# Three pooling inputs and three mixed values of a hybrid decoder layer turned by 32x32 blocks on VectorE and a DRAM detour on GpSimd's DMA queue

## The chip, the cores and the metric

One core of one Trainium2 chip runs the whole program. The metric is the device time of one execution in microseconds (us). The kernel before has a median of 1524.18 us over 3 runs (1524.03 to 1524.83). Everything is float32 at the input and the output.

## What is computed

One layer of a decoder trunk on 256 tokens of 2048 channels. A normalised input is projected into nine parts; two causal mixers work on them, a gated linear attention with 16 heads and a trailing mean over 2, 4, 8 or 16 tokens (one window for each quarter of the channels). Both are gated, summed, projected and added to the input; a gated MLP follows. The part that the change touches:

```python
proj = jnp.einsum('bsd,de->bse', rmsnorm(x, norm_mix_w[l]), w_in[l])
q, k, v, z, b_raw, a_raw, p_in, g_a, g_b = jnp.split(proj, splits, axis=-1)
...
o = gated_delta_rule(q, k, v, g_log, beta)
y_a = rmsnorm(o, gdn_norm_w[l]) * silu(z)
pooled = causal_multiscale_pool(p_in)          # mean over the last 2, 4, 8 or 16 tokens, minus the token
y_b = einsum('bsgc,gcd->bsgd', pooled, pool_w[l]) * pool_scale[l]
mixed = sigmoid(g_a) * y_a + sigmoid(g_b) * y_b
x = x + mixed @ w_out[l]
```

## The kernel before

**Matmuls in split precision.** The program is a long row of matrix products whose weights come from DRAM. A weight tile has 128 partitions and 2 x 512 columns (512 KB). SyncE's queue loads it into `raw` (four buffers). ScalarE casts it to a high part `whi` (L357, three buffers), VectorE subtracts that from `raw` and so makes the low part `wlo` (L368, three buffers). `gemm_a` (L404) then issues twelve matmuls of 128x512 on the tile: for each of two blocks of 128 input channels and each half of the tokens, high times high, low times high, and high times low (L416 to L418). A gemm over all 2048 input channels is eight such tiles, called steps; its result stands in two PSUM tiles, one for each 128 tokens, tokens on the partitions. `weights` (L241) keeps two tiles ahead: when TensorE is given tile n, the loads, casts and splits up to n + 2 have been written.

**The head groups.** The loop at L1245 goes over four groups of 512 channels. Each group has, in this order: K and Q projection (with a scheme that shares products between two column blocks), V, P (the input of the pooling, L1287), gate B, z, the product with `pool_w`, gate A, and the first steps of the next K. The attention's recurrence runs beside them, a piece after each half step (`side`).

**Work that waits for its turn.** What is to be done with a gemm's result is put into the list `later`, and `gemm_a` empties it within the next gemm, ahead of step `flush` (L409 to L411; step 1 in most, step 3 in K and Q). The mixed values have a list of their own, `mixing` (L1235, filled at L1420), which goes into `later` behind K and then Q of the next group. A framework then sets the order on each engine by a simulated timeline; only some stretches are ordered by hand. On the chip each engine works through its list strictly in order.

**The pooling input.** `evict` writes the P gemm, scaled by the norm, to `ev`, tokens on the partitions. The running sums need the tokens along the free axis and the product needs channels on the partitions, so `pooled` (L1306) first turns `ev`: `turned` (L497) makes eight TensorE transposes of 128x128 (L505) into two PSUM tiles `psg`, and two ScalarE copies (L1311) bring them to `pu`. VectorE adds shifted copies (L1319, into `pb` and `pa` in turn, with ScalarE copying the first few tokens, L1318), finishes the mean (L1322 to L1325, `pool`), and the result is split into `phi` (L1327) and `plo` (L1329). For group 3 the windows are applied by matmuls with band matrices instead (`banded`, L1292).

**The mixed values.** `gated` leaves the mixed values of a group in `sz`, tokens on the partitions. The output projection needs channels there. `mixed` (L1413) turns `sz` by eight more transposes, and splits what stands in PSUM into `mhi` (ScalarE, L1416) and `mlo` (VectorE, L1417), one half at a time. For groups 0 to 2 this happens in the next group, for group 3 at the end of the mixers.

**Queues.** Weights go on SyncE's queue (SP). GpSimd (POOL) issues few DMAs in this part of the program and computes a few small things, among them the powers `nk` and `ro` for the norms.

## Time and profile before

| | before |
|---|---|
| median of 3 runs | 1524.18 us (1524.03 to 1524.83) |
| profiled execution, its own time | 1524.25 us |
| its span in the profile | 1522.5 us |
| granted TensorE clock, mean | 0.999 |
| TensorE busy | 1513.1 us, 7260 matmuls and transposes |
| VectorE busy | 1287.0 us |
| ScalarE busy | 896.1 us |
| GpSimd busy | 75.0 us, 97 instructions |

The page of the profile gives each engine's busy time, the span in slices, the chain of work that ended last, and groups of instructions by source line. PE is TensorE, PEld its weight loads, DVE VectorE, ACT ScalarE, POOL GpSimd, SP SyncE. In a row by line stand the line, the engine, the operation, output and input tile, the shape, the count; behind the first bar the busy time and the mean nanoseconds of one; behind the second the idle time ahead of these instructions, and what ended it. In a timeline each row begins with the start and the length in us; `x3` at its end means three such in a row, and a bracket holds the idle time before it and what ended it. A row of DMA issues has the count, the size of one and the median time from issue to landing. In the view by stretch each row has the stretch, its length, the busy time of each engine with its number of instructions, the clock, the share of the DMA engines and the GB/s.

### The profile page before, as it was taken

The numbers are of one execution on the slowest core, as the hardware profiler recorded it, in microseconds if no ns is written. First come the engines' busy times: TensorE is split into PE (matmuls) and PEld (weight loads), VectorE is DVE, ScalarE is ACT, GpSimd is POOL, SyncE is SP. The second block draws the span as 40 slices with busy tenths as digits, with TensorE's granted clock in tenths as the row PEclk, the third lists the DMA queues.
The fourth block names the chain that finished last, engine by engine and source line by source line (L and its number), as shares of the span: only waits on it lengthen the run. The fifth ranks groups of instructions, "written<-read, shape, count | busy, mean of one in ns | idle before, by whom it ended". The sixth has DMA issues, their size and how long they took to land.

```text
span 1522.5 us, 20282 instructions
## 1 busy us (share of the span) xinstructions
PE 1513.1 (99%) x7260; PEld 1250.8 (82%) x7260; DVE 1287.0 (85%) x1799; ACT 896.1 (59%) x1160; POOL 75.0 (5%) x97
## 2 busy tenths in 40 slices
PE   9999999999999999999999999999999999999998
PEld 8888888888878888888888888888888888888886
DVE  6779868888688878888777999999998886989896
ACT  7456556455646456456465676667666665555562
POOL 1000001000100001000000000000000011010100
PEclk9999999999999999999999999999999999999999
DMA  8777647784677747774678656666457468566662
GB/s 277 209 226 221 207 139 225 235 255 115 198 221 218 227 127 219 214 238 154 217 227 303 198 164 218 221 212 216 152 164 238 142 212 276 172 223 219 220 220 100
DMA packets 170099, 313.62 MB, mean 206 GB/s; under 512 B 23650, under 2 KB 27010, under 8 KB 169870
## 3 DMA queue, kind: packets, MB, share of 16 engines
q1 hardware_dynamic: 160864, 283.17, 59.0%
q0 software_dynamic: 7344, 27.27, 5.5%
q10 hardware_dynamic: 1790, 1.89, 0.4%
q8 instruction: 57, 0.93, 0.2%
q14 instruction: 44, 0.36, 0.1%
HBM read 303.33 MB, written 8.95 MB: 205 GB/s over the span
## 4 chain that ended last, share of the span: by engine, by line
PE 98%; DVE 1%; issue 1%; ACT 0%; POOL 0%; POOLq 0%; DVEq 0%
PE psg L455 28%; PE psm L418 14%; PE psm L416 14%; PE psm L417 14%; PE psm L1644 8%; PE psg L1644 7%; PE psm L455 4%; PE psm L606 1%; PE psm L1712 1%; PE psg L505 1%; PE psg L993 1%; DVE wlo L368 1%; PE psg L995 0%; PE psm L521 0%; PE psg L1139 0%
## 5 line engine op out<-in xcount | busy, mean ns | idle before, releaser
L357 ACT CAST whi<-raw 128x1024 fp32r<-128x1024 f32 x400 | 419.9, 1052 | 311.0 <-PE psm L417 157.9
L368 DVE TENSOR_TENSOR wlo<-raw,whi 128x1024 fp32r<-128x1024 f32 x398 | 484.1, 1220 | 119.3 <-ACT whi L357 113.9
L357 ACT CAST whi<-quad 128x1024 fp32r<-128x1024 f32 x217 | 227.9, 1053 | 167.5 <-PE psg L455 46.2
L368 DVE TENSOR_TENSOR wlo<-quad,whi 128x1024 fp32r<-128x1024 f32 x217 | 263.4, 1220 | 39.9 <-ACT whi L357 34.8
L416 PE MATMUL psm<-whi,xhl 128*128 128x512 f32 x384 | 150.0, 391 | 0.0
L417 PE MATMUL psm<-whi,xhl 128*128 128x512 f32 x384 | 149.9, 390 | 0.0
L418 PE MATMUL psm<-wlo,xhl 128*128 128x512 f32 x384 | 139.0, 393 | 0.0
L455 PE MATMUL psg<-whi,fhl 128*128 128x512 f32 x504 | 127.1, 389 | 0.0
L284 DVE TENSOR_TENSOR quad<-quad,quad 128x1024 f32<-128x1024 f32 x92 | 111.9, 1217 | 0.1
L455 PEld LDWEIGHTS psg<-whi,fhl 128*128 128x128 f32 x504 | 94.6, 188 | 19.7
L416 PEld LDWEIGHTS psm<-whi,xhl 128*128 128x128 f32 x384 | 72.1, 188 | 15.0
L417 PEld LDWEIGHTS psm<-whi,xhl 128*128 128x128 f32 x384 | 72.1, 188 | 14.9
L418 PEld LDWEIGHTS psm<-wlo,xhl 128*128 128x128 f32 x384 | 71.7, 188 | 14.6
L455 PE MATMUL psg<-wlo,fhl 128*128 128x512 f32 x252 | 69.8, 389 | 0.0
L455 PE MATMUL psg<-whi,ups 128*128 128x512 f32 x216 | 58.1, 391 | 0.0
L455 PEld LDWEIGHTS psg<-wlo,fhl 128*128 128x128 f32 x252 | 47.3, 188 | 9.9
L1644 PE MATMUL psm<-whi,hhi 128*128 128x512 f32 (+1 forms) x140 | 54.2, 387 | 0.0
L1644 PE MATMUL psm<-whi,hlo 128*128 128x512 f32 (+1 forms) x140 | 53.7, 386 | 0.0
L1644 PE MATMUL psm<-wlo,hhi 128*128 128x512 f32 (+1 forms) x140 | 50.2, 386 | 0.0
L455 PEld LDWEIGHTS psg<-whi,ups 128*128 128x128 f32 x216 | 40.3, 188 | 8.5 <-issue 0.2
L1644 PE MATMUL psg<-whi,hhi 128*128 128x512 f32 (+1 forms) x120 | 46.4, 387 | 0.0
L1644 PE MATMUL psg<-whi,hlo 128*128 128x512 f32 (+1 forms) x120 | 46.1, 386 | 0.0
(495 smaller groups left out, 3001.2 us busy)
## 6 DMA issues: line engine op xcount, KB each, us to landing
raw<-in_w_in_dram SPq DMA_DIRECT2D x212, 512.0 KB, 4.5
raw<-in_w_up_dram SPq DMA_DIRECT2D x104, 512.0 KB, 4.7
quad<-in_w_up_dram SPq DMA_DIRECT2D x72, 512.0 KB, 5.3
raw<-in_w_down_dram SPq DMA_DIRECT2D x56, 512.0 KB, 5.1
quad<-in_w_down_dram POOLq DMA_DIRECT2D x32, 512.0 KB, 5.4
raw<-in_w_out_dram SPq DMA_DIRECT2D x24, 512.0 KB, 3.7
mv<-vrow SPq DMA_DIRECT2D x12, 512.0 KB, 4.9
quad<-in_w_in_dram SPq DMA_DIRECT2D x12, 512.0 KB, 6.8
```

The lines of the kernel that those rows point to most:

```text
L284: nc.vector.tensor_tensor(out_, plus_, minus_, op=ALU.subtract)
L357: last_cast[0] = nc.scalar.copy(hi, raw).ins
L368: last_split[0] = nc.vector.tensor_tensor(lo, raw, hi.bitcast(F32), op=ALU.subtract).ins
L416: mm(ps[:, t, :], lh(k, t), hi[:, kk, :], start=(k == 0), stop=False, **seeded)
L417: mm(ps[:, t, :], ll(k, t), hi[:, kk, :], start=False, stop=False, **seeded)
L418: mm(ps[:, t, :], lh(k, t), lo[:, kk, :], start=False, stop=(k == nk - 1), **seeded)
L455: last_product[0] = mm(ps, lhs(kk), w[n][:, kk], stop=False, skip_group_check=True, start=(first and n == 0 and kk == 0 and lhs is high)).ins
L505: nc.tensor.transpose(pt[:, ff, t * P : (t + 1) * P], src[:, t, f * P : (f + 1) * P], ident)
L606: mm(ps_k0[:, t, :], part(k, t), w[:, kk, :], start=(k == 0 and w is hi and part is xh), stop=(k == KD - 1 and w is lo))
L993: mm(pg0, kq[:, h, 0, 0:P], kq[:, h, :, :], start=True, stop=True)
L1644: mm(ps[:, cs], lhs(kk), part_[:, kk, cs], start=(first and kk == 0 and n == 0), stop=(last and kk == 1 and n == 2), skip_group_check=shared)
L1712: nc.tensor.transpose(out_[f // 2][:, f % 2, t * P : (t + 1) * P], e[:, t, f * P : (f + 1) * P], ident)
```

## The change

A new function turns a tile of 256 tokens x 512 channels without TensorE. VectorE transposes within blocks of 32x32 into `blocks`; one DMA stores `blocks` (512 KB) to a DRAM tile `way`; four DMAs, one for each group of 32 partitions of the target, load the blocks from there in their turned places. All five DMAs are on GpSimd's queue. An element of such a load is a run of 32 floats, 128 bytes, and each load has 32 x 32 = 1024 of them.

```diff
+    def turned_by_dma(src, blocks, dst, queue):
+        nc.vector.transpose(blocks, src)
+        way = dpool.tile([2, P, 512], F32, tag="way", name=nm("way"))
+        queue.dma_start(way.rearrange("t p c -> p t c"), blocks)
+        way = way.rearrange("t (q j) (f a i) -> a j f (t q) i", q=4, a=4, i=32)
+        for a in range(4):
+            queue.dma_start(dst[32 * a : 32 * a + 32].rearrange("j f (u i) -> j f u i", i=32), way[a])
+        return dst
...
         e = evict(ps) if g == 3 else evict(ps, rsh)
+        if g < 3:
+            blocks = mp.tile([P, 2, 512], F32, tag="pa", name=nm("blocks"))
+            u = mp.tile([P, 4, S], F32, tag="pu", name=nm("pu"))
+            turned_by_dma(e, blocks, u, nc.gpsimd)
...
-        def pooled(e=e, g=g, win=win, phi=phi, plo=plo):
-            u = mp.tile([P, 4, S], F32, tag="pu", name=nm("pu"))
-            for f2, pt in enumerate(turned(e)):
-                nc.scalar.copy(u[:, 2 * f2 : 2 * f2 + 2, :], pt)
+        def pooled(u=u, g=g, win=win, phi=phi, plo=plo):
             src, n = u, 1
...
             gated()
+        if g < 3:
+            blocks = mtile(4 + g, [P, 2, 512], F32, nm("blocks"))
+            whole = mp.tile([P, 4, S], F32, tag="sz", name=nm("whole"))
+            turned_by_dma(sz, blocks, whole, nc.gpsimd)
...
         if g < 3:
-            mixing.append(mixed)
+            def parts(whole=whole, mh=mh, ml=ml):
+                nc.scalar.copy(mh, whole)
+                nc.vector.tensor_tensor(ml, whole, mh.bitcast(F32), op=ALU.subtract)
+            mixing.append(parts)
```

In groups 0 to 2 the pooling input is turned right behind its eviction, so `pooled` begins with the sums; and the mixed values are turned as soon as `gated` has written them, into a tile `whole` in the other buffer of `sz`, from which `mhi` and `mlo` are then split as a whole rather than by halves. The buffer of `sz` is also that into which SyncE loads the convolution's taps for V of the next group, and that load moves behind four more weight loads on SyncE's queue. `banded`, and `mixed` of group 3, stay as they are. Line numbers behind the new function are ten higher (L1319 becomes L1329), and some more behind the later edits.

ScalarE's order in group 0, from the last `ga` of the attention's preparation to the split of the pooled values (`whi` are weight tiles, `pu` the turned pooling input, `pb` the first sum, `phi` the high part of the pooled values). Before:

```order
L357 CAST whi_1282<-raw_1280 128x1024
L1015 ACTIVATE ga_126_821<-psg_953,st_826 128x2x128
L1015 ACTIVATE ga_126_821<-psg_966,st_826 128x2x128
L357 CAST whi_1300<-raw_1298 128x1024
L1311 COPY pu_1221<-psg_1222 128x512
L1311 COPY pu_1221<-psg_1227 128x512
L357 CAST whi_1318<-raw_1316 128x1024
L1318 COPY pb_1234<-pu_1221 128x4
L357 CAST whi_1336<-raw_1334 128x1024
L1327 CAST phi_1200<-pool_1237 128x1024
```

The same place after the change:

```order
L357 CAST whi_1278<-raw_1276 128x1024
L1025 ACTIVATE ga_126_821<-psg_953,st_826 128x2x128
L1025 ACTIVATE ga_126_821<-psg_966,st_826 128x2x128
L357 CAST whi_1296<-raw_1294 128x1024
L1328 COPY pb_1230<-pu_1201 128x4
L357 CAST whi_1314<-raw_1312 128x1024
L357 CAST whi_1332<-raw_1330 128x1024
L1337 CAST phi_1209<-pool_1233 128x1024
```

The two copies out of PSUM are gone, and the copy that starts `pb`, which now reads what a DMA brings, stands ahead of the weight tile that it stood behind.

VectorE's order in group 2, at the running sums (`wlo` are the low parts of weight tiles, `pb` and `pa` the sums over two and four tokens and `pb` again over eight). Before:

```order
L368 TENSOR_TENSOR wlo_4328<-raw_4324,whi_4326 128x1024
L368 TENSOR_TENSOR wlo_4375<-raw_4371,whi_4373 128x1024
L368 TENSOR_TENSOR wlo_4393<-raw_4389,whi_4391 128x1024
L1319 TENSOR_TENSOR pb_4355<-pu_4342 128x4x255
L1319 TENSOR_TENSOR pa_4358<-pb_4355 128x4x254
L368 TENSOR_TENSOR wlo_4411<-raw_4407,whi_4409 128x1024
L1319 TENSOR_TENSOR pb_4361<-pa_4358 128x4x252
L368 TENSOR_TENSOR wlo_4429<-raw_4425,whi_4427 128x1024
```

The same place after the change:

```order
L368 TENSOR_TENSOR wlo_4375<-raw_4371,whi_4373 128x1024
L368 TENSOR_TENSOR wlo_4393<-raw_4389,whi_4391 128x1024
L368 TENSOR_TENSOR wlo_4411<-raw_4407,whi_4409 128x1024
L1329 TENSOR_TENSOR pb_4337<-pu_4308 128x4x255
L1329 TENSOR_TENSOR pa_4340<-pb_4337 128x4x254
L368 TENSOR_TENSOR wlo_4429<-raw_4425,whi_4427 128x1024
L1063 COPY tb_4437<-idb 128x256
L1329 TENSOR_TENSOR pb_4343<-pa_4340 128x4x252
```

The number of the same tile is 18 lower now. Two weight tiles more are split ahead of the first sum, and the transpose that feeds it stands earlier, among the splits behind the eviction.

GpSimd's order from the triangular masks `crow` of group 0 to those of group 1 (`nk` and `ro` are the powers for the norms). Before:

```order
L974 AFFINE_SELECT crow_829<-crow_829 128x512 x2
L1003 TENSOR_TENSOR nk_824<-ssk_823,half 128x2x2 x2
L1181 TENSOR_TENSOR ro_1672<-ro_1672,epsx 128x8
L974 AFFINE_SELECT crow_2399<-crow_2399 128x512 x2
L1003 TENSOR_TENSOR nk_2394<-ssk_2393,half 128x2x2 x2
```

The same place after the change:

```order
L984 AFFINE_SELECT crow_829<-crow_829 128x512 x2
L1013 TENSOR_TENSOR nk_824<-ssk_823,half 128x2x2
L514 DMA way_1203<-blocks_1200 128x2x512
L517 DMA pu_1201<-way_1203 32x32x32 x4
L1013 TENSOR_TENSOR nk_824<-ssk_823,half 128x2x2
L1191 TENSOR_TENSOR ro_1668<-ro_1668,epsx 128x8
L984 AFFINE_SELECT crow_2392<-crow_2392 128x512 x2
L514 DMA way_2040<-blocks_2037 128x2x512
L517 DMA whole_2038<-way_2040 32x32x32 x4
L1013 TENSOR_TENSOR nk_2387<-ssk_2386,half 128x2x2 x2
```

Each turn puts one store and four loads into this queue; one `nk` of group 0, and both of group 1, now stand behind such a set.

## The prediction

> **What bounds the kernel now.** I read the page first, then the busy time of each engine by stretch, then the timelines of TensorE, ScalarE and VectorE at the places where the change takes something out. The page says that TensorE works almost without a pause, and that the chain which ended last is TensorE's own:
>
> ```profile
> span 1522.5 us, 20282 instructions
> ...
> PE 1513.1 (99%) x7260; PEld 1250.8 (82%) x7260; DVE 1287.0 (85%) x1799; ACT 896.1 (59%) x1160; POOL 75.0 (5%) x97
> ...
> PE 98%; DVE 1%; issue 1%; ACT 0%; POOL 0%; POOLq 0%; DVEq 0%
> ```
>
> The change lies in the head groups 0 to 2. The view by stretch, cut near the group borders (columns: length, then busy time of PE, PEld, DVE, ACT, POOL, granted clock, share of the DMA engines, GB/s), shows the same for groups 1 and 2:
>
> ```profile
> 285.00:461.00 176.00, 175.86 (x885) 144.41 (x884) 142.99 (x246) 96.86 (x140) 6.90 (x5) 1.00 0.67 201
> 461.00:637.00 176.00, 175.92 (x888) 144.69 (x887) 144.28 (x247) 97.28 (x141) 8.35 (x6) 1.00 0.68 202
> ```
>
> TensorE stands still for about 0.1 us in 176, VectorE has 33 us free, GpSimd is nearly empty. So an instruction that leaves TensorE is worth its full time, provided that the weight tiles keep coming: each must be cast on ScalarE (L357) and split on VectorE (L368) in time, and those two engines work strictly in order. A cast or split that stands behind an instruction waiting for a transfer waits too, and TensorE has some two tiles in hand.
>
> **What leaves TensorE.** Six turns (three of the pooling input, three of the mixed values) of eight transposes each. TensorE's timeline at the first:
>
> ```profile
> 124.16 0.39 PE L418 MATMUL psm<-wlo,xhl2a 128*128 128x512 f32 x1
> 124.39 1.03 PE L505 MATMUL psg<-ident,ev 128*128 128x128 f32 x8
> 125.18 0.47 PE L416 MATMUL psm<-whi,xhl2a 128*128 128x512 f32 x1
> 125.50 0.39 PE L417 MATMUL psm<-whi,xhl2a 128*128 128x512 f32 x1
> ```
>
> Matmuls overlap, so starts count: L418 to the next start takes 0.23, the eight transposes 0.79 (124.39 to 125.18), and the matmul behind them 0.32 instead of 0.23. That is 0.79 + 0.09 = 0.88 us a turn; the busy time of 1.03 is the upper bound. I take 0.87: 6 x 0.87 = **5.2 us gained** (at most 6 x 1.03 = 6.2).
>
> **What VectorE and ScalarE get.** The rows by line:
>
> ```profile
> L1041 DVE STREAM_TRANSPOSE kq<-kq 128x1024 f32<-128x1024 f32 x4 | 4.9, 1236 | 0.0
> L1416 ACT CAST mhi<-psg 128x512 fp32r<-128x512 f32 x8 | 4.3, 580 | 3.7 <-PE psg L505 3.7
> L1417 DVE TENSOR_TENSOR mlo<-psg,mhi 128x512 fp32r<-128x512 f32 x8 | 5.2, 685 | 5.2 <-ACT mhi L1416 5.2
> L1311 ACT COPY pu<-psg 128x512 f32<-128x512 f32 x6 | 3.2, 591 | 2.6 <-PE psg L505 2.6
> ```
>
> VectorE gets six transposes of the size of L1041's: 6 x 1.24 = 7.4 us, and gives back some 0.45 where two halves of mlo (2 x 0.685) become one whole of about 1.22, thrice 0.15. ScalarE loses the six copies of pu (3.5 us). Against 33 us free per group this costs nothing on average; where VectorE is packed (just behind the transpose of group 0) a split may come late by a few tenths. I put 0.4 us in the sum for that, from zero to 1.24 us per turn if no cover held, which is 7.4.
>
> **The new path.** It decides. A turn is now: transpose on VectorE, one store of 512 KB to DRAM, four loads of 128 KB that wait for it, each of 32 partitions x 32 runs of 128 bytes, so 1024 runs, all issued by GpSimd. Rows of issue times, and of landings (median us from issue):
>
> ```profile
> L298 POOL DMA_DIRECT2D quad<-in_w_down_dram x32 | 23.1, 721 | 155.5 <-DVE wlo L368 139.3 <-PE psg L455 16.1 <-issue 0.2
> L1629 POOL DMA_DIRECT2D y<-y x3 | 1.7, 568 | 421.9 <-ACT whi L357 371.6 <-DVE y L1627 50.3
> ```
>
> ```profile
> xtd<-xt POOLq DMA_DIRECT2D x4, 512.0 KB, 4.5
> whole<-y POOLq DMA_DIRECT2D x3, 512.0 KB, 5.4
> TT<-tbd SPq DMA_DIRECT2D x16, 32.0 KB, 1.9
> ```
>
> The store is the twin of xtd: 4.5. A load's issue is not shown at 1024 runs. y is 128 runs of 4 KB (0.568), quad 256 of 2 KB (0.721): 1.2 ns for each more run on 0.41 us fixed, which gives 0.41 + 1024 x 0.0012 = 1.64 us. The bounds: 0.72 if runs are free beyond 256, and 4 x 0.721 = 2.9 if all is proportional. I take 1.64, the line through both rows. The last load still has to land: TT, also from DRAM in 128-byte runs, takes 1.9 from its issue of 0.4, so 1.5 more. A turn takes 0.1 + 4.5 + 4 x 1.64 + 1.5 = **12.7 us** from the end of the transpose; 0.1 + 4.5 + 2.9 + 1.5 = 9.0 and 0.1 + 4.5 + 11.6 + 1.5 = 17.7 at the bounds.
>
> The Trainium skill, "DMA: Bandwidth & Descriptors", section on the anatomy of a DMA on the GpSimd path, calls descriptor generation a small cost that shows late, and gives a DMA 2.0 us plus its bytes at 436 GB/s. An estimate by that page: 3.2 us for the store, 2.3 for the last load, and no reader late, so 1519 us; no run here shows 1024 runs.
>
> **How long the readers can wait.** Group 0, pooling input. ScalarE and VectorE now:
>
> ```profile
> 122.37 1.05 ACT L357 CAST whi<-raw 128x1024 fp32r<-128x1024 f32 x1
> 125.03 1.07 ACT L1311 COPY pu<-psg 128x512 f32<-128x512 f32 x2 [1.60 <-PE psg L505]
> 125.98 1.06 ACT L357 CAST whi<-raw 128x1024 fp32r<-128x1024 f32 x1
> 126.94 0.20 ACT L1318 COPY pb<-pu 128x4 f32<-128x4 f32 x1
> 128.68 1.06 ACT L357 CAST whi<-raw 128x1024 fp32r<-128x1024 f32 x1 [1.54 <-PE psm L417]
> ```
>
> ```profile
> 114.73 3.53 DVE L368 TENSOR_TENSOR wlo<-raw,whi 128x1024 fp32r<-128x1024 f32 x3
> 125.47 1.22 DVE L368 TENSOR_TENSOR wlo<-raw,whi 128x1024 fp32r<-128x1024 f32 x1
> 126.61 1.21 DVE L1319 TENSOR_TENSOR pb<-pu 128x1020 f32<-128x1020 f32 x1
> 127.74 1.22 DVE L368 TENSOR_TENSOR wlo<-raw,whi 128x1024 fp32r<-128x1024 f32 x1
> ```
>
> By the order, the transpose stands behind the first of the three splits at 114.73, so it ends near 115.9 + 1.24 = 117.1. pb's first reader stands on ScalarE behind the cast of 122.37, one place earlier than now, so ScalarE arrives at 123.4 and stops there; on VectorE it keeps its place at 126.6. What is late next is the split at 127.74. whi has three buffers, so the cast at 128.68 marks the end of the tile two before that one; a tile is 12 matmuls of 0.227 = 2.73 us, so TensorE begins the tile of 127.74 at 131.4 and needs its low part with the third matmul, 131.85, or 131.0 once the transposes are gone. VectorE needs pb and that split, 2.4 us, from the landing: it must come by 128.6, **11.5 us** after the transpose.
>
> Group 2, pooling input:
>
> ```profile
> 465.23 0.69 ACT L876 ACTIVATE ev<-psm,rsh 128x512 f32<-128x512 f32 x1
> 477.39 1.05 ACT L357 CAST whi<-raw 128x1024 fp32r<-128x1024 f32 x1 [1.66 <-PE psm L417]
> ```
>
> ```profile
> 465.00 1.23 DVE L368 TENSOR_TENSOR wlo<-raw,whi 128x1024 fp32r<-128x1024 f32 x1 [0.47 <-ACT whi L357]
> 478.48 1.22 DVE L368 TENSOR_TENSOR wlo<-raw,whi 128x1024 fp32r<-128x1024 f32 x1 [0.19 <-ACT whi L357]
> ```
>
> The transpose goes behind the split at 465.00 and ends at 467.4. Its readers pb and pa stand ahead of the split now at 478.48, whose tile was cast at 477.39: that tile begins 2 x 2.73 later, at 482.85, low part at 483.3, less 0.87 = 482.4. Three VectorE instructions (3.4 us) lie between, so the landing must come by 479.0: **11.6 us**.
>
> The other four have more. Mixed values of group 0 and pooling input of group 1:
>
> ```profile
> 237.18 1.22 DVE L941 SCALAR_TENSOR_TENSOR kq<-th,cy 128x1024 f32<-128x1024 f32 x1
> 254.87 1.21 DVE L368 TENSOR_TENSOR wlo<-raw,whi 128x1024 fp32r<-128x1024 f32 x1
> ```
>
> ```profile
> 288.90 1.23 DVE L368 TENSOR_TENSOR wlo<-raw,whi 128x1024 fp32r<-128x1024 f32 x1 [0.26 <-ACT whi L357]
> ```
>
> ```profile
> 306.74 1.05 ACT L357 CAST whi<-raw 128x1024 fp32r<-128x1024 f32 x1 [1.62 <-PE psm L417]
> ```
>
> The mixed transpose goes behind kq, so it ends at 239.6, and its reader on VectorE stands behind the split that ends at 256.1: 16 us, about 18 with the lead of the tiles. Group 1's pooling input: 288.90 + 1.2 + 1.24 = 291.4 to 307.8, again 16 and about 18. The mixed values of groups 1 and 2 have seven tiles between transpose and reader instead of six. Behind the loads on GpSimd's queue stands only the pow for nk, read a gemm later. On SP the load of the taps into sz's buffer moves behind four more weight loads, and there the buffer is free.
>
> **The sum.** Late: 12.7 - 11.5 = 1.2 and 12.7 - 11.6 = 1.1, so 2.3 us given back. -5.2 + 2.3 + 0.4 = -2.5. The profiled execution took 1524.25 (span 1522.5), 0.07 over the median of 1524.18, so 1524.2 - 2.5 = **1521.7 us**.
>
> **The rivals.** A difference under 0.2%, 3.05 us, is no change as far as a measurement of this kernel can tell.
> - All hidden: a load's issue costs little more than quad's 0.72. Then 9.0 us, no wait, -5.2: 1519.0 (1518.0 with the busy time of the transposes). For it: two rows on issue differ little. Against: neither has short runs.
> - Late loads, the slower side: issue is proportional to runs, 2.9 each, 17.7 us a turn. ScalarE and VectorE stop in front of pb in groups 0 and 2, 6.2 + 6.1 = 12.3 us; -5.2 + 12.3 + 0.4 = +7.5: 1531.7. It is slower than no change when 2 x (turn - 11.55) exceeds 4.8 + 3.05, a turn of 15.5, so an issue of 2.35 us or more. For it: GpSimd's issue grows with runs. Against: the growth between the two rows is far from proportional. With the store at 5.4 as well, a turn is 18.6: 14.1, and 0.6 for each of the other four: about 1536.
> - VectorE becomes the bound: all 7.4 us show: 1524.2 - 5.2 + 7.0 = 1526.
> - The turning itself crawls: a turn of 19 times whole's 5.4, 103 us, less 11.5 or 18 of cover, is 2 x 91 + 4 x 85 = 520 us more: about 2040. TT's 1.9 us for 256 runs speaks against it. The Trainium skill, same page, "Rules for kernel authors", gives that factor of 19 for a plain DMA with a rearranged pattern against the hardware's DMA transpose. The block transposes on VectorE make the runs 128 bytes, which that rule does not name.
>
> That the change leaves the transposes in is excluded: the order of TensorE lacks them.
>
> **Chances.** Forecast (turn of 12 to 14.5 us, 1520 to 1526) 0.40; all hidden 0.28; late loads 0.27; VectorE 0.03; crawling 0.02. The forecast's own spread reaches below 1521.1 with 0.14 of its 0.40. Faster 0.28 + 0.14 = 0.42; same 0.26 + 0.03 = 0.29; slower 0.27 + 0.02 = 0.29. The range runs from 1518 (all hidden, busy time) to 1536 (late loads with a slow store).
>
> **What would show it.** Right: 48 fewer L505 matmuls; way landing in 4 to 5 us; GpSimd's four loads at about 1.6 us each; waits of ScalarE for pu of some 4 to 7 us (VectorE about 2) in groups 0 and 2, and TensorE idle there for about 1 us each, nowhere else. Issues under 1 us and no idle TensorE would mean the first rival, issues over 2.4 the second. Wrong altogether: waits in front of mhi or in group 1, late raw tiles at these places (the loads taking the weights' share of the DMA engines), or a TensorE gain other than 0.87 a turn.

## The result and the profile after

The changed kernel takes 1543.65 us (median of 4 runs, 1542.54 to 1546.84) against 1524.11 us before: 1.0132 times as long, with a 95% interval of 1.0119 to 1.0144. Forecast were 1521.7 us and a range of 1518 to 1536. The profiled execution took 1546.84 us, the longest of the four. Its page:

```profile
span 1545.1 us, 20267 instructions
...
PE 1518.6 (98%) x7212; PEld 1249.0 (81%) x7212; DVE 1289.2 (83%) x1802; ACT 893.4 (58%) x1151; POOL 98.8 (6%) x127
...
PE 65%; DMA 2%; DVE 2%; issue 2%; ACT 1%; POOL 0%; POOLq 0%; SPq 0%; DVEq 0%; ACTq 0%
```

TensorE issues 48 instructions fewer and is busy 5.5 us longer; the chain that ended last is TensorE's for 65% of the span instead of 98%. Most of that difference is no reading: the chain is followed back only to the store of a turn at 432 us, so 28% of the span has no entry. DMAs stand on it now, with 2%, and VectorE has 2% instead of 1%. What TensorE waited for in the mixers (us in total, times, longest), which was one wait of 0.2 us before:

```profile
PE psm L418 <- DVE wlo L368: 9.3, 8, 3.0
PE psm L416 <- ACT whi L357: 7.1, 5, 2.7
```

Weight tiles are late. Why they are, ScalarE's and VectorE's waits of the same stretch show:

```profile
ACT whi L357 <- DMA raw<-in_w_in_dram: 39.8, 15, 6.8
ACT mhi L1435 <- DMA whole<-way: 11.8, 3, 5.8
ACT pb L1328 <- DMA pu<-way: 11.0, 2, 8.5
```

```profile
DVE mv L921 <- DMA mv<-vrow: 18.4, 6, 6.7
DVE mlo L1436 <- ACT mhi L1435: 9.0, 3, 4.5
DVE pb L1329 <- DMA pu<-way: 6.3, 2, 5.1
```

Three kinds of wait have grown: for the turned tiles (`pu`, `whole`); for the weight tiles themselves (`raw`, 10.7 us before); and for `mv`, the shifted copies of V, which an older detour through DRAM on SyncE's queue brings for V's convolution (1.3 us before).

The turns themselves, by the lines of the store and of the loads:

```profile
L514 POOL DMA_DIRECT2D way<-blocks x6: 753/774/913, 117.0 to 613.6; - x6
...
DMA to landing us min/median/max: 3.8/5.3/6.7
```

```profile
L517 POOL DMA_DIRECT2D pu<-way x12: 856/964/1104, 123.7 to 490.4; - x12
L517 POOL DMA_DIRECT2D whole<-way x12: 856/969/1109, 252.5 to 621.5; - x12
...
DMA to landing us min/median/max: 3.2/6.6/9.5
```

A load of 1024 runs is issued in 0.97 us, not 1.64, but lands 3.2 to 9.5 us after its issue; the last of the four, which decides, after 5.8 to 9.5. From the end of the block transpose to the last landing the six turns take 15.6, 17.9, 16.3, 18.1, 13.1 and 15.6 us.

**A staircase.** The matmuls of `gemm_a` (L416 to L418) are 2832 in every kernel here, in the same order, so the start of each can be held against its start before. The lag, by the tile (twelve matmuls) that begins there, in us; the columns behind the second are experiments that are told below:

| tile, its start before | changed | pooling only | mixed only | mixed, far readers | detours nobody reads |
|---|---|---|---|---|---|
| 28, 122.3 | +0.2 | +0.9 | +0.1 | +0.6 | +0.2 |
| 36, 145.0 (pooling input 0) | +5.2 | +3.0 | +0.1 | +0.6 | +0.2 |
| 64, 242.6 | +4.8 | +4.8 | -0.7 | -0.2 | +0.2 |
| 80, 292.3 (mixed 0, V of group 1) | +8.0 | +4.8 | +0.4 | +0.4 | +1.5 |
| 92, 325.8 (pooling input 1) | +11.8 | +4.2 | +0.4 | +0.4 | +3.8 |
| 120, 425.0 | +12.5 | +5.8 | -0.6 | -0.5 | +4.9 |
| 136, 474.7 (mixed 1, V of group 2) | +18.0 | +7.6 | +7.7 | -0.5 | +6.2 |
| 148, 507.3 (pooling input 2) | +18.0 | +7.6 | +7.7 | -0.5 | +6.2 |
| 172, 594.3 | +17.9 | +7.1 | +6.8 | -1.4 | +6.4 |
| 188, 644.0 (mixed 2, V of group 3) | +22.5 | +8.4 | +13.0 | -1.4 | +6.4 |
| 212, 723.9 (group 3) | +22.5 | +15.8 | +13.0 | -1.4 | +6.4 |

Behind that nothing is lost. By these rows 13.3 of the changed kernel's 22.5 us lie between the turn of a mixed value and V behind it (3.2, 5.5 and 4.6), and 8.8 at the first two pooling inputs (5.0 and 3.8). The first step of the changed kernel is the one that the prediction named, group 0's pooling input. ScalarE's timeline there:

```profile
122.87 1.04 ACT L357 CAST whi<-raw 128x1024 fp32r<-128x1024 f32 x1
132.41 0.20 ACT L1328 COPY pb<-pu 128x4 f32<-128x4 f32 x1 [8.50 <-DMA pu<-way]
132.51 1.99 ACT L357 CAST whi<-raw 128x1024 fp32r<-128x1024 f32 x2
```

A copy of four columns stands in ScalarE's queue ahead of two casts and holds them for 8.5 us. TensorE's timeline behind it:

```profile
130.51 0.39 PE L418 MATMUL psm<-wlo,xhl 128*128 128x512 f32 x1
133.61 0.80 PE L416 MATMUL psm<-whi,xhl 128*128 128x512 f32 x1 [2.71 <-ACT whi L357]
134.20 0.63 PE L417 MATMUL psm<-whi,xhl 128*128 128x512 f32 x1
134.63 0.63 PE L416 MATMUL psm<-whi,xhl 128*128 128x512 f32 x1
...
139.74 0.40 PE L416 MATMUL psm<-whi,xhl 128*128 128x512 f32 x1
139.98 0.40 PE L417 MATMUL psm<-whi,xhl 128*128 128x512 f32 x1
```

TensorE stops for 2.7 us, and then starts its matmuls every 0.43 us instead of 0.23 for some 6 us, which costs nearly 3 us more. With the pooling alone (`pool_only` below) the same stop lasts 2.4 us, the starts behind it come every 0.23 us, and the step is +2.1 instead of +5.0. The granted clock (the third number from the end) by stretch:

```profile
120.00:130.00 10.00, 10.00 (x46) 8.28 (x45) 7.09 (x16) 2.76 (x4) 4.59 (x5) 1.00 0.82 236
130.00:140.00 10.00, 7.29 (x20) 5.39 (x20) 7.53 (x10) 5.92 (x8) 0.00 (x0) 0.66 0.82 202
```

Group 1's pooling input is another matter. Its readers stand far enough behind, but the weight tile does not come:

```profile
309.78 1.05 ACT L357 CAST whi<-raw 128x1024 fp32r<-128x1024 f32 x1 [1.24 <-DMA raw<-in_w_in_dram]
317.67 1.04 ACT L357 CAST whi<-raw 128x1024 fp32r<-128x1024 f32 x1 [6.85 <-DMA raw<-in_w_in_dram]
```

A `raw` load issued at 307.5 us, with the four loads of the turn in flight, lands after 11.4 us; the longest in the three groups before was 6.9.

At the mixed values TensorE does not stop right behind the waiting reader but 20 to 27 us later, at splits among V's convolution (1.5, 3.0 and 2.8 us in the three groups), each after VectorE has waited for `mv` (4.2, 5.9 and 6.7 us). The chain of work that ended last shows the way there in group 1 (start, length, what):

```profile
440.35 9.40 DMA whole<-way
...
449.86 1.06 ACT mhi L1435
...
454.94 6.46 DMA vrow<-ev
...
461.41 3.63 DMA mv<-vrow
...
468.98 1.15 DVE wlo L368
...
470.17 0.74 PE psm L418 x2
```

The waiting `mhi` holds ScalarE, which evicts V late; V's own detour starts late; VectorE waits for `mv` with a split behind it. The store `vrow<-ev` of that detour, on SyncE's queue, also takes longer: 7.4, 6.5 and 6.8 us to land instead of 3.0, 4.2 and 3.2. In group 2 the chain has V's detour too, but not the mixed reader.

**The buffer of `sz`.** The part on the change says that `whole` lies in the other buffer of `sz`. There is only one, so the load of the taps into it, on SyncE's queue, waits until `mlo` has read `whole` (6.9 us in three waits), and everything behind it on that queue waits too. The prediction's "there the buffer is free" is wrong with it.

### The profile page after: what moved, and what is told of

It is laid out like the page before. It is cut to its first block, busy times and chain, and to the rows that moved or that the text cites. A ratio compares the mean times of both kernels' runs of the same rounds, so it can differ in the third digit from the quotient of the medians.

```text
span 1545.1 us, 20267 instructions
## 1 busy us (share of the span) xinstructions
PE 1518.6 (98%) x7212; PEld 1249.0 (81%) x7212; DVE 1289.2 (83%) x1802; ACT 893.4 (58%) x1151; POOL 98.8 (6%) x127
## 4 chain that ended last, share of the span: by engine, by line
PE 65%; DMA 2%; DVE 2%; issue 2%; ACT 1%; POOL 0%; POOLq 0%; SPq 0%; DVEq 0%; ACTq 0%
PE psg L455 28%; PE psm L1662 7%; PE psg L1662 7%; PE psm L418 6%; PE psm L416 6%; PE psm L417 5%; PE psm L455 3%; PE psm L1730 1%; DVE wlo L368 1%; DMA vrow<-ev 1%; DMA whole<-way 1%; DMA mv<-vrow 1%; DMA crow<-crd 0%; DVE quad L284 0%; PE psg L1003 0%
## 5 line engine op out<-in xcount | busy, mean ns | idle before, releaser
L416 PE MATMUL psm<-whi,xhl 128*128 128x512 f32 x384 | 152.6, 397 | 5.4 <-ACT whi L357 5.4
L417 PE MATMUL psm<-whi,xhl 128*128 128x512 f32 x384 | 152.0, 396 | 0.0
L418 PE MATMUL psm<-wlo,xhl 128*128 128x512 f32 x384 | 140.3, 396 | 2.4 <-DVE wlo L368 2.3
L416 PEld LDWEIGHTS psm<-whi,xhl 128*128 128x128 f32 x384 | 73.6, 192 | 22.2 <-ACT whi L357 6.7
L418 PEld LDWEIGHTS psm<-wlo,xhl 128*128 128x128 f32 x384 | 72.5, 190 | 19.2 <-DVE wlo L368 4.1
L417 PEld LDWEIGHTS psm<-whi,xhl 128*128 128x128 f32 x384 | 73.4, 191 | 15.4
```

The source lines that it names most:

```text
L416: mm(ps[:, t, :], lh(k, t), hi[:, kk, :], start=(k == 0), stop=False, **seeded)
L417: mm(ps[:, t, :], ll(k, t), hi[:, kk, :], start=False, stop=False, **seeded)
L418: mm(ps[:, t, :], lh(k, t), lo[:, kk, :], start=False, stop=(k == nk - 1), **seeded)
```

## The experiments

Each was timed beside the kernel before, whose median was 1523.9 to 1524.6 us. Two theories stood at the start. One says that each step of the staircase belongs to its own turn, and that the loss at the mixed values comes from the taps that wait on SyncE's queue. The rival says that the loss is the traffic of the detours, which delays weight tiles wherever a turn lies. Both changed on the way.

**Pooling alone** (`pool_only`).

```diff
-        if g < 3:
-            blocks = mtile(4 + g, [P, 2, 512], F32, nm("blocks"))
-            whole = mp.tile([P, 4, S], F32, tag="sz", name=nm("whole"))
-            turned_by_dma(sz, blocks, whole, nc.gpsimd)
...
-            mixing.append(parts)
+            mixing.append(mixed)
```

> Only the three pooling inputs are turned by way of DRAM; the mixed values are turned on TensorE as before. The staircase of TensorE's lag behind the kernel before, read off the two traces, has steps of +6.0 (group 0) and +4.8 us (group 1) at the pooling inputs and about 0 in group 2; three turns taken off TensorE give 2.7 back. If each stall belongs to its own turn: +10.8 - 2.7 = +8, about 1532. If the stalls at the pooling inputs owe a good part to TensorE's or SyncE's lag from the mixed values (theory: one chain), group 1's step shrinks and the time is 1527 to 1530. If the loss is spread over the DMA traffic of all six turns alike, half of it is left: about 1534.

1539.95 us, ratio 1.0107 (1.0083 to 1.0132). The staircase shows +8.4 up to group 3. That is the expected sum by luck: the steps are +2.1 in group 0, where +6.0 was expected, none at group 1's pooling input, where +4.8 was, and +1.3 to +1.8 in four other stretches. Then come 7.5 us where nothing is turned: TensorE waits 5.2 us for the solve of group 3's attention. Removing the turns makes the scheduler write another order, and a stop at the same place stands in `nt_pool` below, which has no detour.

**Mixed values alone** (`mixed_only`): the opposite edit.

> Only the three mixed values go by way of DRAM; the pooling inputs are turned on TensorE. In the staircase the stretches from the mixed values to V's convolution cost 3.1, 8.0 and 7.2 us in the profiled run, and three turns off TensorE give 2.7 back: theory one (each stall belongs to its turn, and here to the taps that wait on SyncE's queue for the buffer of sz): +18.3 - 2.7 = +15.6, about 1539, less some 2 since the median lies below the profiled run. Theory two (traffic alike for all six turns): about 1534. Waits of VectorE for mv of 15 us or more under theory one.

1541.45 us, ratio 1.0109 (1.0094 to 1.0125). The staircase has +13.0, so the two halves come near the change's 22.5 (8.4 + 13.0), though not at the same places. VectorE waits for `mv` only 5.9 us. TensorE's loss stands in two stops, both right behind the waiting reader, and ScalarE's timeline ahead of the first shows at what:

```profile
PE psm L416 <- ACT whi L357: 10.7, 2, 6.4
```

```profile
421.65 1.06 ACT L357 CAST whi<-raw 128x1024 fp32r<-128x1024 f32 x1 [0.40 <-PE psm L417]
434.36 1.04 ACT L1435 CAST mhi<-whole 128x1024 fp32r<-128x1024 f32 x1 [11.66 <-DMA whole<-way]
```

ScalarE stands in front of `mhi` for 11.7 us, with the casts behind it. This turn took 22.6 us from the end of the block transpose to the landing; 4.1 of them passed before its store, which stood in GpSimd's queue behind the masks:

```profile
413.63 2.21 POOL L984 TENSOR_SCALAR_AFFINE_SELECT crow<-crow 128x512 f32<-128x512 f32 x2 [11.74 <-DMA crow<-crd]
415.78 0.78 POOL L514 DMA_DIRECT2D way<-blocks  x1
```

**Another buffer** (`whole_in_pu`).

```diff
-            whole = mp.tile([P, 4, S], F32, tag="sz", name=nm("whole"))
+            whole = mp.tile([P, 4, S], F32, tag="pu", name=nm("whole"))
```

> The whole change, but the turned mixed values go to the buffer of pu, which is idle then, rather than to the only buffer of sz; so the load of the taps on SyncE's queue no longer waits for the whole detour, and the weight tiles and the V detour behind it neither. Theory one (queue blocked behind the taps): VectorE's wait for mv falls from 18.4 to about 2 us, and most of the 18 us between the mixed values and V's convolution goes: 1527 to 1531. Theory two (the 128-byte traffic makes the weight tiles late): nothing changes, 1541 to 1545.

1547.67 us, ratio 1.0150 (1.0130 to 1.0170). VectorE's wait for `mv` falls to 7.0 us, and the time does not: ScalarE waits 58.5 us for `raw` instead of 39.8. The taps held SyncE's queue (V's store lands after 3.1 to 4.7 us now), but freeing it gains nothing; the first theory of the mixed values falls.

**No turn at all** (`no_turn`).

```diff
+            u = e.rearrange("p t (f i) -> p (t f) i", f=2)
...
+            def parts(whole=sz.rearrange("p t (f i) -> p (t f) i", f=2), mh=mh, ml=ml):
```

> Left out: the six turns of groups 0 to 2 altogether, by either way; the sums and the split of the mixed values read the unturned tile. This is the ceiling of any way to take the turns off TensorE. The prediction's 0.87 us a turn gives -5.2: 1519.0. If the transposes cost TensorE only where they delay the next matmul for other reasons (a tile that is late anyway), less than -3; if ScalarE's copies and VectorE's halves also cost, more than -6.

1522.20 us (median of 10), ratio 0.9989 (0.9979 to 0.9998). Taking the turns off TensorE is worth 2 us, not 5.2. In the staircase the step of 0.9 us is there at single turns (tile 28 to 32 goes from +0.2 to -0.7), but other places give it back: in the order that goes with it VectorE waits 7.5 us for `mv` and 11.2 us for the solve's input, against 1.3 and 0.5 before. The profiled execution, at 1520.38 us, is the fastest of the ten, so its staircase shows more gain than the median.

**Readers written later** (`late_readers`, and `late_pool` with the pooling alone).

```diff
-        tb = gate(gemm_a(xh, xl, KD), "th")
+        tb = gate(gemm_a(xh, xl, KD, flush=5 if g < 3 else 1), "th")
...
-                later.extend(mixing)
-                mixing.clear()
+                if not kind:
+                    later.extend(mixing)
+                    mixing.clear()
```

> The whole change with the turned mixed values in pu's buffer, and the readers of all turns later: the sums of the pooling input start at step 5 of the gate B gemm instead of step 1 (4 tiles of 2.73 us, 10.9 us), the split of the mixed values stands in the V gemm instead of the Q gemm (some 13 us later). Theory R (readers stand too near to turns of 13 to 23 us): no waits for pu and whole are left, 1522 to 1526, near the kernel without any turn (1522.2). Theory T (the turns' own traffic makes weight tiles late, whoever reads): ScalarE's waits for raw tiles stay (58 us with whole in pu against what the kernel without turns has, 24), and the time stays above 1530.

> Only the pooling inputs by way of DRAM, their sums started at step 5 of the gate B gemm. Theory R: the steps of +2.1 and +2.5 us that the staircase shows at groups 0 and 2 for the pooling inputs alone go, the turns taken off TensorE give 1 to 2.7 back: 1522 to 1524. Theory T: the waits for pu go but raw tiles still come late, 1530 or more.

1543.23 us (ratio 1.0133, 1.0105 to 1.0160) and 1543.11 us (1.0120, 1.0102 to 1.0137). These runs do not test what they were made for. The scheduler places a reader where its simulation has the data: the order of `late_readers` is that of `whole_in_pu` row for row on every engine and queue, and that of `late_pool` is that of `pool_only`. So they are repeats, and show what a repeat is worth in these kernels: 1547.67 and 1543.23 us for one order, 1539.95 and 1543.11 for the other. A difference of 3 to 4 us between two kernels that wait for late transfers, four runs each, tells nothing by itself.

**The detour that nobody reads** (`cost_alone`): the kernel before, and four detours besides.

```diff
+        if g < 2:
+            blocks = mtile(5 + g, [P, 2, 512], F32, nm("blocks"))
+            ux = mtile(1 + g, [P, 4, S], F32, nm("ux"))
+            turned_by_dma(e, blocks, ux, nc.gpsimd)
...
+        if g < 2:
+            blocks = mtile(5 + g, [P, 2, 512], F32, nm("blocks"))
+            whole = mtile(1 + g, [P, 4, S], F32, nm("ux"))
+            turned_by_dma(sz, blocks, whole, nc.gpsimd)
```

> The kernel before, with all turns on TensorE, and besides the four detours of groups 0 and 1 (block transpose on VectorE, store, four loads) into idle tiles that nobody reads: the detour's cost without its gain and without a reader. Theory R: nothing waits, and only VectorE's 4 x 1.24 us and GpSimd's order can show: 1524 to 1527. Theory T: the traffic alone makes weight tiles late in both groups: 1530 to 1537, with ScalarE waiting for raw as in the changed kernel.

1530.55 us, ratio 1.0038 (1.0024 to 1.0052); the staircase has +6.3. With no reader, all turns still on TensorE and nearly the order of the kernel before (six of 7260 rows on TensorE stand elsewhere), a third or so of the loss is there. ScalarE's timeline in group 1 has the same late tile as the changed kernel:

```profile
304.37 1.05 ACT L357 CAST whi<-raw 128x1024 fp32r<-128x1024 f32 x1 [0.99 <-DMA raw<-in_w_in_dram]
311.64 1.04 ACT L357 CAST whi<-raw 128x1024 fp32r<-128x1024 f32 x1 [6.23 <-DMA raw<-in_w_in_dram]
```

**The same with runs of 2 KB** (`cost_alone_long`).

```diff
-        way = way.rearrange("t (q j) (f a i) -> a j f (t q) i", q=4, a=4, i=32)
+        way = way.rearrange("t p c -> p t c")
         for a in range(4):
-            queue.dma_start(dst[32 * a : 32 * a + 32].rearrange("j f (u i) -> j f u i", i=32), way[a])
+            queue.dma_start(dst[32 * a : 32 * a + 32].rearrange("p (t f) s -> p t (f s)", t=2), way[32 * a : 32 * a + 32])
```

> Cost_alone with one change: the four loads of a detour are plain copies in runs of 2 KB instead of 128 bytes (the block is not turned; nobody reads it). The order on TensorE, VectorE and ScalarE is the same row for row. If the bytes on the DMA engines are what delays the weight tiles: 1529 to 1531 as cost_alone. If the short runs do: 1524 to 1526.

1526.33 us (median of 10), ratio 1.0017 (1.0007 to 1.0026). Between 3 and 4 of the 6 us go with the short runs, in the very same order of TensorE and VectorE. The landings of weight tiles in the three groups, with short runs and with long ones:

```profile
DMA to landing us min/median/max: 3.5/4.2/13.1
```

```profile
DMA to landing us min/median/max: 3.5/4.2/8.6
```

The median is that of the kernel before; a few tiles that meet the four loads are late. Late tiles alone do not point to a detour, though: `nt_both` below has none and has weight tiles that land after up to 9.4 us, and `far_mixed` has some of 10.6 us without loss. The Trainium skill, "DMA: Bandwidth & Descriptors", section on queues, rings and completion order, says that each DMA engine finishes a whole packet of one queue before it turns to the next. That fits a weight tile that waits behind GpSimd's packets; the runs show the late tiles, not the engine's turns.

**The turn by itself** (`by_itself`): a chain of turns, quiet and beside a stream of weight tiles.

```diff
+        for _ in range(6):
+            h = short_turn(h)
+        for _ in range(6):
+            h = long_turn(h)
```

> Not the layer at all: left out is everything but turns, 24 of them in a chain. First 6 detours with runs of 128 bytes and 6 with the same store and four plain loads of 2 KB runs while nothing else moves; then the same 12 while SyncE streams weight tiles of 512 KB at the layer's pace, one per 2.7 us of ScalarE casts. Theory one (sharing with the weight tiles makes a turn long): with nothing else a turn takes 9 to 11 us (store 3 to 4.5, last load about 2), with the stream 13 to 18, and 2 KB runs suffer from the stream as 128 byte runs do. Theory two (short runs are slow by themselves): 13 us or more already with nothing else, and the 2 KB loads are several us faster in both stretches.

VectorE's rows: the bracket is the time from one block transpose to the next, first quiet, then beside the stream:

```profile
36.96 1.25 DVE L71 STREAM_TRANSPOSE blocks<-shorts 128x1024 f32<-128x1024 f32 x1 [9.61 <-DMA shorts<-way]
48.04 1.25 DVE L71 STREAM_TRANSPOSE blocks<-shorts 128x1024 f32<-128x1024 f32 x1 [9.84 <-DMA shorts<-way]
...
180.88 1.25 DVE L71 STREAM_TRANSPOSE blocks<-shorts 128x1024 f32<-128x1024 f32 x1 [14.99 <-DMA shorts<-way]
196.81 1.25 DVE L71 STREAM_TRANSPOSE blocks<-shorts 128x1024 f32<-128x1024 f32 x1 [14.69 <-DMA shorts<-way]
```

Quiet, a turn takes 9.6 to 9.8 us (store 3.2, loads 2.9 to 3.4); beside the stream 14.7 to 18.2 (store 4.3 to 7.7, loads 4.6 to 8.5). Loads in 2 KB runs land in 2.6 to 3.1 quiet and 4.7 to 6.9 beside it, so the stream, not the run length, makes a turn long. The stream ran denser than the layer's: the DMA engines were 96% busy, at 282 GB/s.

**Readers queued by hand** (`far_mixed`, `far_pool`, `far_readers` with both).

```diff
-                later.extend(mixing)
-                mixing.clear()
...
         later.append(lambda e=e, g=g, vt2=vt2: v_moved(e, g, vt2))
+        later.extend(mixing)
+        mixing.clear()
...
         def pooled(u=u, g=g, win=win, phi=phi, plo=plo):
+            with tc.issue_after(last_split[0]), tc.issue_after(last_cast[0]):
...
-        tb = gate(gemm_a(xh, xl, KD), "th")
+        tb = gate(gemm_a(xh, xl, KD, flush=9 if g < 3 else 1), "th")
...
-            whole = mp.tile([P, 4, S], F32, tag="sz", name=nm("whole"))
+            whole = mp.tile([P, 4, S], F32, tag="pu", name=nm("whole"))
...
             def parts(whole=whole, mh=mh, ml=ml):
+                with tc.issue_after(last_split[0]), tc.issue_after(last_cast[0]):
```

`far_pool` has the lines at `pooled` and `tb`, `far_mixed` the others.

> Only the mixed values by way of DRAM, into pu's buffer, their split queued by hand behind a weight tile of the P gemm, 9 or 10 tiles after the block transpose in place of 6 or 7. R: the gaps of 6.4 and 4.3 us on TensorE in front of a weight tile behind mhi go: 1522 to 1524. R and T: the steps of 1.3 us per group at V's convolution that the unread detour shows stay: 1525 to 1528. Neither: 1540.

> Only the pooling inputs by way of DRAM, their sums queued behind the first split of the z gemm. R: 1522 to 1524 up to group 3. R and T: the step of +2.3 us that the unread detour shows in group 1 stays, 1525 to 1527. The pooling-only kernels so far have a stall of 7.5 us in group 3, at the solves of the attention, where nothing is turned; if the scheduler's order there is the same again, it comes on top.

> Late_readers left the order as it was: the scheduler puts a reader where its simulated timeline has the data, wherever it is written. Here the readers are queued by hand behind weight tiles: the sums of the pooling input behind the split that stands first in the z gemm, the split of the mixed values behind one in the P gemm, so 8 tiles (21.8 us) or more after the block transpose on VectorE, in place of 4 to 7; the turned mixed values lie in pu's buffer. Theory R (waiting readers are the loss): their waits go, and most of the 19 us with them, 1522 to 1525. Theory R and T (the detours nobody reads cost 6 us for four, so 9 for six; the rest is readers): 1524.4 + 9 - 2 to 4 = 1529 to 1531. Neither: 1540.

`far_mixed`: 1524.33 us (median of 10), ratio 1.0004 (0.9995 to 1.0013). The 17 us of `mixed_only` are gone to the last, although its detours are even longer (21.1 to 26.2 us to the landing, 16.3 to 22.6 in `mixed_only`). TensorE's waits are those of the kernel before:

```profile
PE psg L505 <- ACT ev L886: 0.3, 1, 0.3
PE psm L418 <- DVE wlo L368: 0.2, 1, 0.2
```

`far_pool`: 1531.39 us, ratio 1.0053 (1.0038 to 1.0068). `far_readers`: 1540.85 us, ratio 1.0113 (1.0097 to 1.0130), though ScalarE's waits for turned tiles are down to 2.5 us in all. So with the mixed values alone the loss came with the waiting readers, and three detours that nobody waits for cost next to nothing. (`far_mixed` also has the buffer of `whole_in_pu`, and 24 rows on TensorE stand elsewhere than in `mixed_only`; neither was taken apart from the readers.) For the pooling input, and for both together, something else is left.

**Longer runs there** (`far_pool_long`, `far_readers_long`, `after_long`): the loads of `cost_alone_long` in `far_pool`, `far_readers` and the changed kernel.

> Far_pool with its four loads as plain copies in runs of 2 KB instead of 128 bytes; the block is then not turned, so the pooled values are others. The order is the same row for row on TensorE, VectorE, ScalarE and SyncE's queue. Short runs hold up the weight tiles (theory S): the 7.5 us that far_pool still loses shrink by the share that the unread detour showed (4.2 of 6.1 us), to 1525 to 1527. Bytes or the order alone: 1530 to 1532.

> Far_readers with the four loads of each of the six detours in runs of 2 KB (not turned, other values). The scheduler orders some hundred rows otherwise here, so only a large difference counts. S: the raw tile that landed 13.5 us after its issue among the short loads of group 2 lands in 5 to 9, ScalarE's wait for raw falls from 57 us towards 25 to 35, and the time from 1540.9 to 1526 to 1532. If it stays above 1538, the runs' length is not what keeps the loss when nobody waits for a turn.

> The changed kernel with the four loads of each detour in runs of 2 KB (not turned, other values), its readers where the scheduler puts them. A load is issued in 0.55 instead of 0.97 us and lands a little earlier, so a detour takes 11 to 15 us instead of 13 to 18. If waiting readers are most of the loss and the short runs the rest: 1530 to 1536. If the short runs were all of it: 1524 to 1526; if they are nothing: 1542 to 1545.

1532.62 us (ratio 1.0059, 1.0044 to 1.0074), 1532.43 us (1.0053, 1.0038 to 1.0068) and 1540.04 us (1.0109, 1.0092 to 1.0126). In the pooling's own order the run length is nothing; with both detours and far readers it may be 8 us, in an order that differs too; with the readers where the scheduler puts them it is less than a repeat tells (1540.04 against 1543.65).

**The order without detours** (`nt_mixed`: `far_readers` without the pooling detours; `nt_pool`: `far_pool` without them; `nt_both`: no detour at all).

```diff
-            turned_by_dma(e, blocks, u, nc.gpsimd)
...
+                u = e.rearrange("p t (f i) -> p (t f) i", f=2)
...
-            turned_by_dma(sz, blocks, whole, nc.gpsimd)
+            nc.vector.transpose(blocks, sz)
+            whole = blocks.rearrange("p t (f i) -> p (t f) i", f=2)
```

> Far_readers without the three pooling detours: the sums read the unturned pooling input (other values), queued behind the z gemm's first split as there; the mixed values keep their detours and late readers. The order differs from far_readers in 4 rows on TensorE and 49 on VectorE. If the pooling detours' traffic is what far_readers still loses (1540.9): 1522 to 1526. If the order is, in which the attention stands 2 to 3 tiles later than in the kernel before: 1534 to 1541. Both: between.

> Far_pool without its detours: the pooling input is not turned at all (other values), its sums queued as there, the mixed values turned on TensorE; nothing goes by way of DRAM that did not before. It differs from far_pool in about 700 of 6888 rows on TensorE. Order alone as the cause of far_pool's 7.5 us: 1530 to 1532. The detours' traffic as the cause: 1521 to 1525.

> Nt_mixed without the last detours: the mixed values are block-transposed on VectorE and split from there (not turned, other values), queued behind the same weight tiles. No turn goes by way of DRAM or TensorE; the order differs from nt_mixed in 174 of 6864 rows on TensorE and 54 of 1802 on VectorE. Nt_mixed is at 1536.2. Order alone: 1533 to 1537 here too. Detours in that order: 1521 to 1525, as the kernel without turns whose sums the scheduler places (1522.2).

`nt_both` 1530.66 us (ratio 1.0051, 1.0034 to 1.0068), `nt_mixed` 1536.24 (1.0078, 1.0063 to 1.0093), `far_readers` 1540.85: in nearly the same order, no detour costs 6.4 us against the kernel before, the mixed detours add 5.6 and the pooling detours 4.6. For `nt_both` order alone was expected at 1533 to 1537 and the detours alone at 1521 to 1525; it lies between. Four runs each make these steps rough. `nt_pool` takes 1536.08 us (1.0080, 1.0063 to 1.0097) with nothing turned by DMA; 8 us of it are one stop in group 3:

```profile
PE psg L1113 <- DVE T L1089: 6.2, 1, 6.2
```

So an order made around a later pooling costs several us by itself. Whether the order of the changed kernel does so too is open: no run has exactly that order without its detours. Only `no_turn`, which leaves the turns out and computes other values, is ahead of the kernel before, by 2 us.

## Why the prediction was wrong

Three things in the sum failed: how long a turn takes, how far the four readers stand that were to be safe, and what the turns do to other transfers, which was put at nothing.

- **The step that failed first** is "the last load still has to land: TT ... takes 1.9 from its issue of 0.4, so 1.5 more", together with the store as "the twin of xtd: 4.5". `TT` is a load of 32 KB, a quarter of the size. The last 128 KB load landed 5.8 to 9.5 us after its issue, the store after 3.8 to 6.7. By itself the last load takes 3.3 us and the store 3.2, and beside a stream of weight tiles they take about as long as in the layer, so most of the miss is the weight tiles in the same DMA engines.
- **The disputed cost was the wrong one.** The issue of 1024 runs took 0.97 us and came every 0.78; the forecast's 1.64 was on the high side, and the range that was built on it (0.72 to 2.9) spread the turn in the right region, 9.0 to 17.7, for a wrong reason. The turns took 13.1 to 18.1.
- **"The other four have more"** failed for the three mixed values, and that cost the most (13.3 of the staircase's 22.5 us). Their readers waited in all three groups (2.6, 5.9 and 3.3 us at `mhi`). ScalarE came to `mhi` 15.4, 12.3 and 12.3 us after the block transpose, not 16 to 19: the distance was reckoned in tiles at TensorE's pace, but in groups 1 and 2 the mixed values are ready 3.4 tiles later in the new order (when TensorE is at tile 118.0 instead of 114.6, and 172.0 instead of 168.6), as in `pool_only` and not in `mixed_only`, and six casts then follow within 12.3 us. With the mixed values alone, moving the readers takes the loss away (1541.45 to 1524.33). In the changed kernel the wait reaches TensorE through V's detour, by the chain in group 1, and moving the readers there does not take the loss away (`far_readers`, 1540.85).
- **What was left out** is that the loads delay others: weight tiles (11.4 us to land in group 1), and with them SyncE's queue, where the V detour and the taps stand. The prediction named late raw tiles only among the signs that it was wrong altogether. Four unread detours alone cost 6 us in the order of the kernel before, so this is a term of its own, of some 1.5 us a turn there; in `far_mixed` three cost no more than the turns taken off TensorE gave back.
- **"5.2 us gained"** was mis-sized: 2.0 (0.3 to 3.2 by the interval of `no_turn`). The 0.9 us a turn is in the staircase; other waits give most of it back.
- **A stop costs more than itself.** Group 0's 2.7 us of idle TensorE became 5.6, which the forecast of "idle there for about 1 us" did not reckon with. The place and the two engines that wait were right, but TensorE stopped for ScalarE's cast behind `pb`, not for VectorE's split; ScalarE waited 8.5 us instead of 4 to 7, VectorE 5.1 instead of 2. In group 2 they waited 2.5 us or less and TensorE not at all.
- **The rival "late loads"** had the sign, and the place in group 0, but its cause was slow issue, and its bound of 1536 lacked the delayed weight tiles, most of the waits at the mixed values, and the slower clock.

Open is how the 19.5 us of the changed kernel divide between readers, traffic and order for the pooling input: taking away one cause alone (`whole_in_pu`, `far_readers`, `after_long`) moves the time by 3 to 4 us at most, which is no more than a repeat does.

## What to carry to other kernels

Price a detour through DRAM by what it takes beside the kernel's own traffic, not by the quiet or small transfer of the same form, and keep its readers behind at least that much work; with the mixed values alone that took 17 us away. Then price what the detour does to others on the same DMA engines and on the in-order queues, as a copy that nobody reads shows. And where a scheduler makes the order, look at the order before timing a reader that was written later: it may not have moved, or the whole order may have. And measure one order twice before reading a few us between two kernels.

## What the runs showed of the hardware

- After a stop of 2.7 us TensorE ran at half speed for 6 us (a start every 0.43 us instead of 0.23), after stops of 2.05 us in group 1 and 3.0 us at 470 us the mean clock of the next 10 us was 0.83; a stop of 2.8 us at 650 us was not followed by any drop, nor was the one of 2.4 us in `pool_only`. The stretches at a granted clock of 0.50 last 6.8 us in the first case and 3.4 in the next two. The Trainium skill, "TensorE: Matmul & The Clock Gate", Part 1, has the clock halved after an idle window of about 3.4 us that runs freely, and 426.7 ns from start to start for 512 columns then. The 0.43 us agree; here stops shorter than the window were enough. A free-running window would let equal stops differ, as these do; that it is the reason is not shown.
- GpSimd issued a load of 1024 runs of 128 bytes in 0.85 to 1.10 us, a load of 64 runs of 2 KB in 0.54 to 0.56.
- Quiet, runs of 128 bytes and of 2 KB landed nearly alike (2.9 to 3.4 and 2.6 to 3.1 us for 128 KB).
